# Two of the four operand sums made by adding transfers, with one quarter kept negated, in a one-core streaming-encoder block

## The chip, the cores and the metric

The kernel runs on one core of a Trainium2 chip. The metric is device time in microseconds (us) of one execution. Engine names follow the profile: PE is TensorE (matmul; PEld its weight loads), DVE is VectorE, ACT is ScalarE, POOL is GpSimd, SP is SyncE, which here only issues transfers. A transfer issued from SP is described by hardware, one issued from POOL by software, and only POOL's can add to their destination.

## The reference

One layer on x of 1024 tokens by 1024 channels, in float32, cut to what is computed:

```python
h = rmsnorm(x, norm_g)
q, k, v, za, u, vs, zs, gm = split(h @ w_in)
a   = window_sink_attention(rope(q), rope(k), v, sinks)
a   = (a * silu(za)) @ w_att_out
sgo = chunked_spatial_gating(gelu(u), gelu(vs), sg_w, sg_b, ln_g, ln_b)
sgo = (sgo * silu(zs)) @ w_sg_out
ga, gs = split(sigmoid(gm + b_merge))
out = rmsnorm(x + (ga * a + gs * sgo) @ w_o, final_g)
```

Below, "s" is the operand sgo * silu(zs) of w_sg_out, and "a" is the operand a * silu(za) of w_att_out. Both are matrices of 1024 by 1024.

## The kernel before, in words

**Products.** Every large product of a 1024 by 1024 operand goes by a seven-product scheme on halves (a Strassen scheme in Winograd's form). The operand is cut in four quarters q11, q12, q21, q22, and seven forms are made of them: b11, b21, b22 are quarters, t1 to t4 are sums of quarters. The other side, the weights, is cut and summed in the same way for each pair of 128-wide output blocks. Each float32 factor is split into a rounded high part and a remainder, and a product takes three matmuls (high by high, high by remainder, remainder by high) over four 128-blocks of the contraction: 12 matmuls of 128x512. `gemm_pair` (line 351) does one pair of output blocks with 7 x 12 = 84 matmuls, in the order b11, t1, t2, b21, t3, b22, t4. b11, t2, t3 and t4 go on in one PSUM bank (ps_mm): b11's product is copied out (the first x<-ps_mm copy, line 360), and then t2 is accumulated on top; so t2 can't start before that copy. t1 and b22 share a bank (ps_o) in the same way, with the copy of line 364 between them; b21 has its own (ps_tp).

**Splits.** `split` (line 147) has ScalarE round to the high part (a CAST, or an ACTIVATE with -1 where a form is negated) and VectorE subtract to get the remainder. A form of s or a is split by `fill_b` (line 179) in two halves of 128x1024 (tiles T_b11h, T_b11l and so on; each has one buffer). The weights of each pair are split into wh and wl, three buffers each, by `split_next` at set places of `gemm_pair`.

**Forms of s and a.** `forms_of` (line 1458) makes the seven forms of an operand whose quarters lie in the four bq tiles (128x4x512 each). It makes four sums on VectorE by `combine` (line 183), in place and in two halves each:

```python
combine(nc.vector.tensor_sub, q12, q11, q12)   # t1
combine(nc.vector.tensor_add, q12, q22, q12)   # t2, used with a minus sign
combine(nc.vector.tensor_sub, q11, q12, q11)   # t3
combine(nc.vector.tensor_sub, q21, q12, q21)   # t4
```

**Stages around the change.** Four pairs of h by za's weights come first (the stage called za here, starting at about 591 us; its last pair starts at 647.67). While they run, their outputs pass SiLU, are multiplied with the attention's output from at_dr (`finish_silu`, line 1550) and are stored to a_dr; and s is finished: zs is loaded, passes SiLU and is multiplied with rows of s1_dr (`parts_of_s`, line 1492, where a table of pair and hook sets what is done when; each pair has seven hooks). The first sum of s is made before the last za pair, the other forms during it, and four pairs of s by w_sg_out follow (from 666.71). During these, the quarters of a are loaded from a_dr, the outputs are multiplied with the sigmoid gate and stored to y_dr, and in the last pair the forms of a are made. Four pairs of a by w_att_out follow (from 748.56), and then the product with w_o by token.

**Gates.** The att gates (rows of at_dr) and the sigmoid gates (gs_dr, ga_dr) pass through 128x512 tiles named g0 to g3, one buffer each. In the za stage g0 and g1 hold att gates, and g2 and g3 hold rows of s1_dr for s.

**Order.** The program is written in one order, and a scheduler that estimates durations then sets each engine's instruction order, which the engine keeps to strictly. `after(second, first)` fixes an order between two instructions without a wait. Transfers from SP are issued in that queue's order, each behind the waits of those before it. In the za and s stages POOL's queue holds the stores to a_dr and y_dr.

Of the kernel before, what the change touches and what calls it, by code (L numbers as in the profile page):

```python
# [27 lines left out]
ALU = mybir.AluOpType  # L28
# [5 lines left out]
KC = D // P  # L34
# [18 lines left out]
def hybrid_tile(  # L53
# [16 lines left out]
    nc = tc.nc  # L70
# [55 lines left out]
    at_dr = scratch("at_dr")  # L126
# [3 lines left out]
    def rstd_of(ss, scale, base=EPS, n=1):  # L130
# [14 lines left out]
        nc.vector.tensor_mul(e[:], e[:], r0[:])  # L145
        return e

    def split(hi, lo, src, minus=False):
        if minus:
            nc.scalar.mul(hi, src, -1.0)  # L150
            nc.vector.scalar_tensor_tensor(
                lo, src, -1.0, hi.bitcast(F32), op0=ALU.mult, op1=ALU.subtract
            )
        else:
            nc.scalar.copy(hi, src)  # L155
            return nc.vector.tensor_sub(lo, src, hi.bitcast(F32))  # L156

    def after(second, first):

        tc.add_manual_dep(  # L160
            second.ins,
            first.ins.name,
            mybir.DependencyInfo(mybir.DependencyClass.NoSync, mybir.DependencyReason.DATA),
            reason="order",
        )
# [9 lines left out]
    def new_b(names=FORMS):  # L175
        return {n: (slot(n + "h"), slot(n + "l")) for n in names}

    def fill_b(b, name, src, minus=None):
        hi, lo = b[name]
        for c in range(0, 4, 2):  # L180
            split(hi[:, c : c + 2, :], lo[:, c : c + 2, :], src[:, c : c + 2, :], name == "t2" if minus is None else minus)

    def combine(op, dst, a, c):
        for i in range(0, 4, 2):
            op(dst[:, i : i + 2, :], a[:, i : i + 2, :], c[:, i : i + 2, :])  # L185

# [9 lines left out]
    def add_to(dst, src):  # L196
        nc.gpsimd.dma_start(dst, src, accum_op=ALU.add)

    def copy_to(dst, src):
        nc.sync.dma_start(dst, src)  # L200

    def begin_job():
        n = len(begun)
        if n < written[0]:
            begun.append(n)
            units.extend(jobs[n]())

    def split_next():

        if not units:  # L210
            begin_job()
        if not units:
            return
        halves, keys = units.pop(0)
        if keys[0][1] == 2:
            make_sums(term_of_x11[0] if done[0] <= 4 else None)
        hi = mtile([P, D], F32R, "wh", 3)
        lo = mtile([P, D], F32R, "wl", 3)
        if isinstance(halves, list):
            for c, half in enumerate(halves):  # L220
                split(hi[:, half_of(c)], lo[:, half_of(c)], half)
        else:
            wide = halves.shape[1]
            first = split(hi[:, 0:wide], lo[:, 0:wide], halves)
            if keys[0] == (done[0] - 1, 6) and done[0] > LAST_OF_Q + 2:
                make_sums(first)
        for c, key in enumerate(keys):
            ready[key] = hi[:, half_of(c)], lo[:, half_of(c)]
        if len(units) == 1:
            begin_job()  # L230

    def half_of(half):
        return slice(half * HALF, (half + 1) * HALF)
# [19 lines left out]
    def make_sums(first=None):  # L253

        while sums_to_make:
            sums_to_make.pop(0)(first)
# [73 lines left out]
    term = [None]  # L330
# [198 lines left out]
    casts, lows, turns = [], [], []  # L529
# [80 lines left out]
    def two_k(v, c):  # L610
        return v[:, 2 * c : 2 * c + 2, :]
# [131 lines left out]
    for c in range(2):  # L743
        hi, lo = (two_k(v, c) for v in s1_hl)
# [659 lines left out]
    QUARTERS = ((0, 0), (0, 1), (1, 0), (1, 1))  # L1404
# [51 lines left out]
            yield b  # L1456

    def forms_of(qs):
        q11, q12, q21, q22 = (qs[k] for k in QUARTERS)
        b = {}  # L1460

        def fill(name, q):
            b.update(new_b((name,)))
            fill_b(b, name, q)

        combine(nc.vector.tensor_sub, q12, q11, q12)
        yield
        fill("b11", q11)
        fill("t1", q12)
        combine(nc.vector.tensor_add, q12, q22, q12)  # L1470
        fill("t2", q12)
        fill("b21", q21)
        combine(nc.vector.tensor_sub, q11, q12, q11)
        fill("t3", q11)
        fill("b22", q22)
        combine(nc.vector.tensor_sub, q21, q12, q21)
        fill("t4", q21)
        yield b

    ORDER = ((0, 0), (1, 1), (0, 1), (1, 0))  # L1480
    gates = []

    turn = [0]

    def gtag(among=4):
        turn[0] += 1
        return f"g{turn[0] % among}"

    def want_gate(src, m, half, among=4):
        gates.append(get(src, m, half, 1, gtag(among)))  # L1490

    def parts_of_s():

        factors, of_rows = [], {}

        def rows(src, j, half):
            return src[:].rearrange("(c p) t -> p c t", p=P)[:, 4 * j : 4 * j + 4, half_of(half)]

        def load(j, half):
            s_q[j, half] = q = bq()
            copy_to(q[:], rows(z_dr, j, half))

# [12 lines left out]

        def load_row(c, half):
            of_rows[c, half] = get(s1_dr, 4 + c, half, 1, f"g{2 + c % 2}")

        def multiply_row(c, half):
            v = s_q[1, half][:, c, :]
            after(nc.vector.tensor_mul(v, v, of_rows[c, half][:]), term[0])

        return {
            (0, 1): [(load, 0, 0), (load_factors, 0, 0)],
            (0, 2): [(load, 1, 1)],
            (0, 3): [(load, 0, 1)],
            (0, 4): [(load_row, 0, 1), (load_row, 1, 1)],
            (0, 5): [(silu, 0, 0)],  # L1530
            (0, 6): [(multiply, 0, 0, 0)],
            (0, 7): [(multiply, 0, 0, 2), (load_factors, 0, 1), (silu, 1, 1)],
            (2, 1): [(multiply_row, 0, 1), (multiply_row, 1, 1), (load_row, 2, 1), (load_row, 3, 1)],
            (2, 3): [(silu, 0, 1)],
            (2, 6): [(multiply, 0, 1, 0), (multiply_row, 2, 1)],
            (2, 7): [(multiply, 0, 1, 2), (multiply_row, 3, 1), (load, 1, 0), (load_row, 0, 0), (load_row, 1, 0)],
            (4, 6): [(silu, 1, 0)],
            (4, 7): [(multiply_row, 0, 0), (multiply_row, 1, 0), (load_row, 2, 0), (load_row, 3, 0)],
            (6, 6): [(multiply_row, 2, 0), (multiply_row, 3, 0)],
        }  # L1540


    of_att = [(m + i, half) for m in range(0, KC, 2) for i, half in ORDER]
# [5 lines left out]

    def finish_silu(q, m, half):  # L1550

        after(nc.vector.tensor_mul(q[:], q[:], gates.pop(0)[:]), term[0])
        put(a_dr, m, half, q[:], nc.gpsimd)
        if of_att:
            want_gate(at_dr, *of_att.pop(0), 2)

    def part_of_s(m):
        of_za[0] += 1
# [5 lines left out]
    for m in range(0, KC, 2):  # L1564
        if m == 0:
            for _ in range(2):
                want_gate(at_dr, *of_att.pop(0), 2)
        if m == 6:
            s_forms = forms_of(s_q)
            next(s_forms)  # L1570

        def finish(i, half, q, src, sign):
            pace[0] = nc.scalar.activation(q[:], src, AF.Silu, scale=sign)
            silus.append((q, m + i, half))

        gemm_pair(hb, finish, lambda: part_of_s(m), "tp")
# [4 lines left out]

    def gate_of(src, m, i, half, col):

        g = gates.pop(0)
        c = col + m + i
        gate = nc.scalar.activation(g[:], g[:], AF.Sigmoid, bias=bm_sb[:, c : c + 1])

        after(gate, pace[0])
        return g
# [110 lines left out]
    fill = o_forms()  # L1700
# [211 lines left out]
```

## Time and profile before

| | us |
|---|---|
| median of three runs | 911.89 (910.78 to 914.15) |
| profiled execution, its own time | 912.14 |
| its span | 910.4 |
| TensorE busy | 894.2 |
| VectorE busy | 696.8 |
| ScalarE busy | 527.0 |
| POOL busy | 141.9 |

The mean granted TensorE clock of the profiled execution is 0.996. A timeline row gives start, duration, engine, line, operation, output and input, count (merged rows have x2), and in brackets the idle time of the engine before it and what ended that. Matmul records overlap, as they are pipelined: the distance between two starts says how fast they go, not the duration. Rows of windows give the busy time of each engine in a stretch with the count of instructions, then the granted clock, the share of the 16 transfer engines that was busy, and GB/s. A row of grouped instructions gives line, engine, operation, tiles, shape and count, then busy time and mean ns of one, then idle time before it. Rows of transfers end with the median us from issue to landing, where that is known.

### The profile page before, as it was taken

Reading aid. Unit: us, or ns where it says so; the run is one execution under the profiler, and the core shown is the slowest. Engines: PE = TensorE matmul, PEld = TensorE weight load, DVE = VectorE, ACT = ScalarE, POOL = GpSimd, SP = SyncE. Lnnn points to the kernel's source line nnn. Section 1 sums busy time; section 2 is a strip of 40 time slices with the busy share of each in tenths; the row PEclk is TensorE's granted clock in tenths of the full one; section 3 lists DMA queues with packets and bytes.
Section 4 is the critical chain, followed back from the end, with each engine's and each line's share of the span. In section 5 each row is a group of like instructions: output and inputs, shape, how many; then the busy total and the mean of one; then the engine's idle time right before and its main releaser. Section 6 shows DMA issues by size and latency. Waiting matters only on the chain.

```text
span 910.4 us, 13184 instructions
## 1 busy us (share of the span) xinstructions
PE 894.2 (98%) x4284; PEld 743.6 (82%) x4284; DVE 696.8 (77%) x1263; ACT 527.0 (58%) x1059; POOL 141.9 (16%) x204
## 2 busy tenths in 40 slices
PE   8999999999999999999999999999998999999996
PEld 6778888888878788888888888888877887888885
DVE  6869966666676788888878788657797489579986
ACT  7866533334545467767667677654674375367443
POOL 1322222203030001111111011201001111110012
PEclk9999999999999999999999999999999999999999
DMA  9997888858778767788786789899859665998632
GB/s 329 211 250 214 263 204 175 173 153 270 252 235 290 206 181 216 208 178 202 170 239 215 244 224 244 212 345 347 295 192 368 220 197 156 312 307 274 204 120 112
DMA packets 131598, 209.57 MB, mean 230 GB/s; under 512 B 12649, under 2 KB 61033, under 8 KB 131530
## 3 DMA queue, kind: packets, MB, share of 16 engines
q1 hardware_dynamic: 110072, 149.74, 49.7%
q0 software_dynamic: 21312, 58.73, 28.4%
q8 instruction: 34, 0.56, 0.3%
q14 instruction: 34, 0.28, 0.1%
q10 hardware_dynamic: 146, 0.27, 0.1%
HBM read 147.74 MB, written 86.11 MB: 257 GB/s over the span
## 4 chain that ended last, share of the span: by engine, by line
PE 87%; DVE 7%; DMA 2%; issue 1%; ACT 1%; SPq 0%; POOL 0%; DVEq 0%; ACTq 0%
PE ps_mm L342 36%; PE ps_o L342 26%; PE ps_sc L1242 3%; PE ps_tp L342 3%; PE ps_mm L669 3%; PE ps_tp L669 2%; PE ps_o L1327 2%; PE ps_sc L342 2%; PE ps_tp L1286 2%; PE ps_o L669 2%; PE ps_tp L917 2%; PE ps_sc L669 1%; DVE wl L156 1%; DVE bq L185 1%; DMA q_hl<-qhl 1%
## 5 line engine op out<-in xcount | busy, mean ns | idle before, releaser
L155 ACT CAST wh<-s 128x1024 fp32r<-128x1024 f32 (+1 forms) x79 | 79.2, 1005 | 96.0 <-PE ps_mm L342 52.0
L156 DVE TENSOR_TENSOR wl<-wr,wh 128x512 fp32r<-128x512 f32 (+1 forms) x77 | 72.0, 936 | 51.8 <-ACT wh L155 51.0
L156 DVE TENSOR_TENSOR wl<-s,wh 128x1024 fp32r<-128x1024 f32 (+1 forms) x79 | 92.5, 1171 | 12.3 <-ACT wh L155 12.1
L155 ACT CAST wh<-wr 128x512 fp32r<-128x512 f32 (+1 forms) x77 | 63.0, 820 | 58.4 <-PE ps_mm L342 30.4
L342 PE MATMUL ps_o<-T_t1h,wh 128*128 128x512 f32 x148 | 58.8, 397 | 0.8 <-ACT wh L155 0.7
L342 PE MATMUL ps_o<-T_b22h,wh 128*128 128x512 f32 x148 | 58.3, 394 | 0.0
L342 PE MATMUL ps_mm<-T_b11h,wl 128*128 128x512 f32 x140 | 55.4, 396 | 2.9 <-DVE wl L156 2.9
L342 PE MATMUL ps_o<-T_b22l,wh 128*128 128x512 f32 x148 | 57.9, 391 | 0.0
L342 PE MATMUL ps_o<-T_b22h,wl 128*128 128x512 f32 x148 | 57.7, 390 | 0.0
L342 PE MATMUL ps_o<-T_t1h,wl 128*128 128x512 f32 x148 | 57.7, 390 | 0.0
L342 PE MATMUL ps_o<-T_t1l,wh 128*128 128x512 f32 x148 | 57.6, 389 | 0.0
L1255 ACT ACTIVATE pr<-ps_sc,sm 128x192 f32<-128x192 f32 (+2 forms) x128 | 50.9, 410 | 9.0 <-DVE sm L1251 6.6
L342 PE MATMUL ps_mm<-T_b11h,wh 128*128 128x512 f32 x140 | 55.3, 395 | 0.0
L342 PE MATMUL ps_mm<-T_t4h,wh 128*128 128x512 f32 x140 | 55.3, 395 | 0.0
L342 PE MATMUL ps_mm<-T_t2h,wh 128*128 128x512 f32 x140 | 54.7, 391 | 0.6 <-ACT x L360 0.6
L342 PE MATMUL ps_mm<-T_t3l,wh 128*128 128x512 f32 x140 | 54.6, 390 | 0.6 <-DVE T_t3l L156 0.6
L342 PE MATMUL ps_mm<-T_b11l,wh 128*128 128x512 f32 x140 | 55.2, 394 | 0.0
L342 PE MATMUL ps_mm<-T_t3h,wh 128*128 128x512 f32 x140 | 54.9, 392 | 0.0
L342 PE MATMUL ps_mm<-T_t4h,wl 128*128 128x512 f32 x140 | 54.7, 391 | 0.0
L342 PE MATMUL ps_mm<-T_t3h,wl 128*128 128x512 f32 x140 | 54.7, 390 | 0.0
L342 PE MATMUL ps_mm<-T_t2h,wl 128*128 128x512 f32 x140 | 54.6, 390 | 0.0
L342 PE MATMUL ps_mm<-T_t2l,wh 128*128 128x512 f32 x140 | 54.6, 390 | 0.0
(389 smaller groups left out, 2395.2 us busy)
## 6 DMA issues: line engine op xcount, KB each, us to landing
wr<-in_w_dram SPq DMA_DIRECT2D x86, 256.0 KB
sums<-in_w_dram POOLq DMA_DIRECT2D x20, 512.0 KB, 6.7
s<-sums SPq DMA_DIRECT2D x20, 512.0 KB
q_hl<-qhl SPq DMA_DIRECT2D x16, 512.0 KB
q<-q_hl SPq DMA_DIRECT2D x64, 128.0 KB
y_dr<-x POOLq DMA_DIRECT2D x28, 256.0 KB, 6.5
g<-in_w_dram POOLq DMA_DIRECT2D x12, 512.0 KB, 6.0
wr<-in_w_dram SPq DMA_DIRECT2D x11, 512.0 KB
```

The costliest lines, as they stand in the source:

```text
L155: nc.scalar.copy(hi, src)
L156: return nc.vector.tensor_sub(lo, src, hi.bitcast(F32))
L185: op(dst[:, i : i + 2, :], a[:, i : i + 2, :], c[:, i : i + 2, :])
L342: nc.tensor.matmul(acc, lt, rt, start=fresh and k == 0 and n == 0, stop=k == 3 and n == 2, skip_group_check=True,)
L669: mm = nc.tensor.matmul(acc[:], lt, rt, start=fresh and k == 0 and n == 0, stop=k == 3 and n == 2, skip_group_check=True,)
L917: nc.tensor.matmul(pm[:, t * P : (t + 1) * P], xh[:, half * 4 + t, g * P : (g + 1) * P], bias[-1][1][:, g % 4, :], start=True, stop=True,)
L1242: nc.tensor.matmul(sc[:, i, k0:], q_of[:, c, i * P : (i + 1) * P], kt[:, f, k0:], start=f == 0, stop=f == 1,)
L1255: nc.scalar.activation(held_in[c, i], sc[:, i, lo:hi], AF.Exp, bias=nmax[:, c, i : i + 1], scale=-1.0, accum_out=sums[:, c, i : i + 1],)
L1286: nc.tensor.transpose(dst, pr[:, i, block * P : block * P + width], ident[:])
L1327: nc.tensor.matmul(po[:, cs], lt, rt, start=n == 0, stop=n == len(terms) - 1)
```

## The change

In `forms_of`, two of the four sums leave VectorE. t2's sum q12 + q22 and t4's sum are made by transfers on POOL's queue that add one SBUF tile to another, in halves of 128x1024 (`add_aside`, by `add_to`, the same helper that adds into y_dr). So that t4's sum q12 - q21 is an addition, q21 is kept negated from where it is multiplied: in `parts_of_s` for the quarter (1, 0) of s, in `finish_silu` for that of a. The new `times` multiplies with -1 in the same instruction. b21 is then split with a minus sign. The order of the forms changes: b21 is made before t2; the subtraction for t3 is put after t2's remainder, and t2's casts after a cast of the weights, by `after`.

The gate tiles g0 to g3 are handed out from a list of free ones in place of a running number. g2 and g3 join it for att gates at the second hook of the last za pair (`more_gates`), and the last two row products of s move there from that pair's sixth hook.

```diff
+    def times(v, by, minus):
+        if minus:
+            return nc.vector.scalar_tensor_tensor(v, v, -1.0, by, op0=ALU.mult, op1=ALU.mult)
+        return nc.vector.tensor_mul(v, v, by)

     def forms_of(qs):
-        q11, q12, q21, q22 = (qs[k] for k in QUARTERS)
+        q11, q12, minus21, q22 = (qs[k] for k in QUARTERS)
...
+        def add_aside(dst, src):
+            for i in range(0, 4, 2):
+                add_to(dst[:, i : i + 2, :], src[:, i : i + 2, :])
...
         fill("b11", q11)
         fill("t1", q12)
-        combine(nc.vector.tensor_add, q12, q22, q12)
-        fill("t2", q12)
-        fill("b21", q21)
-        combine(nc.vector.tensor_sub, q11, q12, q11)
+        add_aside(q12, q22)
+        fill("b21", minus21, True)
+        lows = fill("t2", q12)
+        for hi in hi_of[-2:]:
+            after(hi, of_units[-2])
+        add_aside(minus21, q12)
+        for sub in combine(nc.vector.tensor_sub, q11, q12, q11):
+            after(sub, lows[-1])
         fill("t3", q11)
         fill("b22", q22)
-        combine(nc.vector.tensor_sub, q21, q12, q21)
-        fill("t4", q21)
+        fill("t4", minus21)
...
-            after(nc.vector.tensor_mul(v, v, of_rows[c, half][:]), term[0])
+            after(times(v, of_rows[c, half][:], half == 0), term[0])
+
+        def more_gates():
+            free_tags.extend(("g2", "g3"))
+            for _ in range(2):
+                want_gate(at_dr, *of_att.pop(0))
...
-            (6, 6): [(multiply_row, 2, 0), (multiply_row, 3, 0)],
+            (6, 2): [(multiply_row, 2, 0), (multiply_row, 3, 0), (more_gates,)],
...
-        after(nc.vector.tensor_mul(q[:], q[:], gates.pop(0)[:]), term[0])
+        after(times(q[:], next_gate()[:], m >= KC // 2 and half == 0), term[0])
```

In the instruction order that results, VectorE has eight instructions fewer in all for the sums (four for s, four for a), and POOL eight adding transfers more. On TensorE, nine of the twelve b21 matmuls of the first s pair go before its t2 matmuls, and ahead of the first pair's t4 go five matmuls of the second pair's b11, where there were twelve of its b11, b21 and t1, for s and for a. On ScalarE, the casts of T_b21h go before those of T_t2h, and the casts of T_b22h and T_t4h go before those of T_t3h; in both stages T_t4h's casts now stand ahead of the first pair's copies out of ps_mm (b11) and ps_o (t1).

More of the change, by code (lines that the diff above doesn't have):

```diff
@@ L146, in rstd_of @@
         return e
+    hi_of = []
     def split(hi, lo, src, minus=False):
         if minus:
-            nc.scalar.mul(hi, src, -1.0)
-            nc.vector.scalar_tensor_tensor(
+            hi_of.append(nc.scalar.mul(hi, src, -1.0))
+            return nc.vector.scalar_tensor_tensor(
                 lo, src, -1.0, hi.bitcast(F32), op0=ALU.mult, op1=ALU.subtract
@@ L154, in split @@
         else:
-            nc.scalar.copy(hi, src)
+            hi_of.append(nc.scalar.copy(hi, src))
             return nc.vector.tensor_sub(lo, src, hi.bitcast(F32))
@@ L179, in fill_b @@
         hi, lo = b[name]
-        for c in range(0, 4, 2):
-            split(hi[:, c : c + 2, :], lo[:, c : c + 2, :], src[:, c : c + 2, :], name == "t2" if minus is None else minus)
+        minus = name == "t2" if minus is None else minus
+        return [
+            split(hi[:, c : c + 2, :], lo[:, c : c + 2, :], src[:, c : c + 2, :], minus) for c in range(0, 4, 2)
+        ]
     def combine(op, dst, a, c):
-        for i in range(0, 4, 2):
-            op(dst[:, i : i + 2, :], a[:, i : i + 2, :], c[:, i : i + 2, :])
+        return [op(dst[:, i : i + 2, :], a[:, i : i + 2, :], c[:, i : i + 2, :]) for i in range(0, 4, 2)]
     jobs = []
@@ L206, in begin_job @@
             units.extend(jobs[n]())
+    of_units = []
     def split_next():
@@ L226, in split_next @@
                 make_sums(first)
+        of_units.append(hi_of[-1])
         for c, key in enumerate(keys):
@@ L1458, in forms_of, with fill @@
     def forms_of(qs):
-        q11, q12, q21, q22 = (qs[k] for k in QUARTERS)
+        q11, q12, minus21, q22 = (qs[k] for k in QUARTERS)
         b = {}
-        def fill(name, q):
+        def fill(name, q, minus=None):
             b.update(new_b((name,)))
-            fill_b(b, name, q)
+            return fill_b(b, name, q, minus)
+        def add_aside(dst, src):
+            for i in range(0, 4, 2):
+                add_to(dst[:, i : i + 2, :], src[:, i : i + 2, :])
         combine(nc.vector.tensor_sub, q12, q11, q12)
@@ L1469, in forms_of, with gtag, want_gate, next_gate @@
         fill("t1", q12)
-        combine(nc.vector.tensor_add, q12, q22, q12)
-        fill("t2", q12)
-        fill("b21", q21)
-        combine(nc.vector.tensor_sub, q11, q12, q11)
+        add_aside(q12, q22)
[6 more added lines that the diff above has]
+            after(sub, lows[-1])
         fill("t3", q11)
         fill("b22", q22)
-        combine(nc.vector.tensor_sub, q21, q12, q21)
-        fill("t4", q21)
+        fill("t4", minus21)
         yield b
+    def times(v, by, minus):
+        if minus:
+            return nc.vector.scalar_tensor_tensor(v, v, -1.0, by, op0=ALU.mult, op1=ALU.mult)
+        return nc.vector.tensor_mul(v, v, by)
     ORDER = ((0, 0), (1, 1), (0, 1), (1, 0))
     gates = []
[L1483 to L1490, printed above, removed]
+    free_tags = ["g0", "g1"]
+    def gtag():
+        tag = free_tags.pop(0)
+        free_tags.append(tag)
+        return tag
+    def want_gate(src, m, half):
+        tag = free_tags.pop(0)
+        gates.append((tag, get(src, m, half, 1, tag)))
+    def next_gate():
+        tag, g = gates.pop(0)
+        free_tags.append(tag)
+        return g
     def parts_of_s():
@@ L1550, in finish_silu @@
     def finish_silu(q, m, half):
-        after(nc.vector.tensor_mul(q[:], q[:], gates.pop(0)[:]), term[0])
+        after(times(q[:], next_gate()[:], m >= KC // 2 and half == 0), term[0])
         put(a_dr, m, half, q[:], nc.gpsimd)
         if of_att:
-            want_gate(at_dr, *of_att.pop(0), 2)
+            want_gate(at_dr, *of_att.pop(0))
     def part_of_s(m):
@@ L1566, in hybrid_tile @@
             for _ in range(2):
-                want_gate(at_dr, *of_att.pop(0), 2)
+                want_gate(at_dr, *of_att.pop(0))
         if m == 6:
@@ L1582, in gate_of @@
     def gate_of(src, m, i, half, col):
-        g = gates.pop(0)
+        g = next_gate()
         c = col + m + i
```

## The prediction

> **What bounds the kernel now.** I read the page first: busy times and the chain of work that ended last.
>
> ```profile
> PE 894.2 (98%) x4284; PEld 743.6 (82%) x4284; DVE 696.8 (77%) x1263; ACT 527.0 (58%) x1059; POOL 141.9 (16%) x204
> PE 87%; DVE 7%; DMA 2%; issue 1%; ACT 1%; SPq 0%; POOL 0%; DVEq 0%; ACTq 0%
> ```
>
> TensorE bounds the whole, so time can only be won where it waits. The changed code makes the seven operand forms of s (used from 667 us on) and of a (from 749 us on), so next I read these two stretches: by windows, then TensorE's timeline.
>
> ```profile
> core 0: us, PE busy (x) PEld busy (x) DVE busy (x) ACT busy (x) POOL busy (x), PEclk, DMA share, GB/s
> 655.00:665.00 10.00, 10.00 (x46) 8.29 (x45) 10.00 (x11) 7.84 (x11) 0.54 (x1) 1.00 0.61 214
> 665.00:675.00 10.00, 10.00 (x46) 8.29 (x45) 8.90 (x12) 6.02 (x9) 1.62 (x3) 1.00 0.71 222
> 675.00:685.00 10.00, 9.37 (x41) 7.04 (x39) 10.00 (x10) 9.06 (x12) 0.00 (x0) 1.00 0.64 237
> 685.00:695.00 10.00, 7.54 (x26) 5.57 (x25) 9.28 (x12) 2.44 (x4) 1.62 (x3) 0.83 1.03 390
> 735.00:745.00 10.00, 10.00 (x46) 8.29 (x45) 9.64 (x12) 9.83 (x14) 0.54 (x1) 1.00 0.44 156
> 745.00:755.00 10.00, 10.00 (x46) 8.29 (x45) 10.00 (x11) 5.95 (x8) 1.63 (x3) 1.00 0.77 247
> 765.00:775.00 10.00, 8.84 (x38) 6.68 (x37) 8.85 (x11) 2.60 (x3) 3.51 (x4) 1.00 0.74 200
> ```
>
> In both stretches VectorE is full (10.00 of 10 us) before TensorE has its holes.
>
> ```profile
> 647.67 0.39 PE L342 MATMUL ps_mm<-T_b11h,wh 128*128 128x512 f32 x1
> 666.71 0.39 PE L342 MATMUL ps_mm<-T_b11h,wh 128*128 128x512 f32 x1
> 679.33 0.50 PE L342 MATMUL ps_mm<-T_t3l,wh 128*128 128x512 f32 x1 [0.63 <-DVE T_t3l L156]
> 686.00 0.50 PE L342 MATMUL ps_o<-T_t1h,wh 128*128 128x512 f32 x1 [0.71 <-ACT wh L155]
> 688.48 0.79 PE L342 MATMUL ps_mm<-T_b11h,wl 128*128 128x512 f32 x1 [1.75 <-DVE wl L156]
> 691.62 0.40 PE L342 MATMUL ps_mm<-T_t4l,wh 128*128 128x512 f32 x1
> 710.48 0.39 PE L342 MATMUL ps_mm<-T_b11h,wh 128*128 128x512 f32 x1
> 748.56 0.39 PE L342 MATMUL ps_mm<-T_b11h,wh 128*128 128x512 f32 x1
> 767.85 0.50 PE L342 MATMUL ps_mm<-T_b11h,wl 128*128 128x512 f32 x1 [1.10 <-DVE wl L156]
> 788.38 0.39 PE L342 MATMUL ps_mm<-T_b11h,wh 128*128 128x512 f32 x1
> ```
>
> A pair of output blocks is 84 matmuls. The last undisturbed one before the s forms runs from 647.67 to 666.71: 19.04 us, 0.2267 us a matmul. The first two pairs on the s forms start at 666.71 and end at 710.48: 43.77 us where two pairs take 38.08. So **5.69 us** are lost there. The first two on the a forms take 788.38 - 748.56 = 39.82 us: **1.74 us** lost. Together 7.43 us, which caps what the change can win. Part of it is the clock: from 688.48 to 691.62 seven matmul starts take 3.14 us instead of 1.59, and the windows show a granted clock of 0.83.
>
> **What ends these waits** is the VectorE backlog.
>
> ```profile
> L185 DVE TENSOR_TENSOR bq<-bq,bq 128x1024 f32<-128x1024 f32 x8 | 9.6, 1217 | 0.0
> L151 DVE SCALAR_TENSOR_TENSOR T_t2l<-bq,T_t2h 128x1024 fp32r<-128x1024 f32 x2 | 2.3, 1215 | 0.0
> 652.15 2.36 DVE L156 TENSOR_TENSOR T_b11l<-bq,T_b11h 128x1024 fp32r<-128x1024 f32 x2 [0.49 <-ACT T_b11h L155]
> 658.89 0.68 DVE L372 TENSOR_TENSOR x<-x,ps_tp 128x512 f32<-128x512 f32 x1
> 672.91 0.69 DVE L1552 TENSOR_TENSOR x<-x,g 128x512 f32<-128x512 f32 x1 [1.01 <-DMA g<-at_dr]
> 687.21 1.22 DVE L156 TENSOR_TENSOR wl<-wr,wh 128x1024 fp32r<-128x1024 f32 x1
> 736.73 2.36 DVE L156 TENSOR_TENSOR T_t1l<-bq,T_t1h 128x1024 fp32r<-128x1024 f32 x2 [0.36 <-ACT T_t1h L155]
> 740.74 0.68 DVE L372 TENSOR_TENSOR x<-x,ps_tp 128x512 f32<-128x512 f32 x1
> 766.58 1.21 DVE L156 TENSOR_TENSOR wl<-wr,wh 128x1024 fp32r<-128x1024 f32 x1
> ```
>
> The weight remainder wl that TensorE awaits at 688.48 is made at 687.21, at 767.85 the one made at 766.58; each stands in VectorE's order behind all of the forms' work.
>
> **The change, part by part.** Spacing on VectorE is 1.14 us for 128x1024 (two take 2.36) and about 0.60 for 128x512 (0.68 as in 658.89's row, less the same overlap of 0.08).
>
> (1) Removed: of the eight sums of each set of forms (four sums in two halves) four leave VectorE, 4 x 1.14 = 4.6 us for s and 4.6 us for a. The s wl of 687.21 then comes at 682.6 or earlier, and TensorE, undisturbed, needs it at 666.71 + (72 + 2) x 0.2267 = 683.5. The a wl of 766.58 comes at about 764.5, behind ScalarE's cast; it is wanted at 748.56 + 74 x 0.2267 = 765.3. Both holes close.
>
> (2) The gate loads. Two more buffers for the att gates from the second hook of the last za pair end the 1.01 us wait at 672.91, and four 128x512 row products move from about 667 to 653. The SP queue gets the same loads in another order; the two of s<-sums move behind gate loads:
>
> ```profile
> 670.20 0.53 SPq L200 DMA_DIRECT2D s<-sums  x1
> ```
>
> What they bring is first wanted at 666.71 + 96 x 0.2267 = 688.5, for t1 of the second pair, 18 us later. Nothing, by this cover; without it, each us of lateness over 10 or so would stall TensorE as long.
>
> (3) Negation: multiply with -1 and split with minus sign are a SCALAR_TENSOR_TENSOR in place of a TENSOR_TENSOR: 1215 beside 1217 ns. Nothing.
>
> (4) Added: eight adding transfers of 512 KB between SBUF tiles on POOL's queue. The same kind and size runs four times in the first stage:
>
> ```profile
> T_t3h<-T_t4h POOLq DMA_DIRECT2D x2, 512.0 KB, 6.9
> T_t3l<-T_t3h POOLq DMA_DIRECT2D x2, 512.0 KB, 4.9
> xh<-xh POOLq DMA_DIRECT2D x4, 256.0 KB, 10.1
> DMA to landing us min/median/max: 4.8/5.6/7.5
> 24.00:28.00 4.00, 4.00 (x23) 3.35 (x23) 2.57 (x8) 3.25 (x8) 0.86 (x1) 1.00 1.05 299
> 32.00:37.00 5.00, 5.00 (x25) 3.96 (x23) 4.27 (x13) 3.80 (x9) 1.81 (x3) 1.00 0.79 152
> ```
>
> From issue to landing L is 4.8 to 7.5 us (the fourth line is that of tile T_t3h, all four). The window with a DMA share of 1.05 holds the slowest, that of 0.79 the two fast ones. I take L = 6, near the mean of the four ((2 x 6.9 + 2 x 4.9) / 4 = 5.9); the ends are 4.8 and 7.5.
>
> (5) The order this brings. The changed instruction order puts ScalarE's two casts of t4, which need the second adding sum, ahead of x<-ps_mm, the copy of the b11 product that TensorE awaits before t2. That is the new wait.
>
> ```profile
> 664.01 1.05 ACT L155 CAST wh<-s 128x1024 fp32r<-128x1024 f32 x1 [0.54 <-ACT x L1573]
> 664.96 1.99 ACT L155 CAST T_b22h<-bq 128x1024 fp32r<-128x1024 f32 x2
> 669.84 0.58 ACT L360 COPY x<-ps_mm 128x512 f32<-128x512 f32 x1
> 748.71 1.05 ACT L155 CAST wh<-s 128x1024 fp32r<-128x1024 f32 x1
> ```
>
> ScalarE spaces such casts by 0.95 us (two take 1.99). For s: from 664.01 come wh, two t2, wh, two b22 (six casts) and two activations of 0.5, then t4 twice: the second may start at 671.7. After it follow t3 and the copy: 671.7 + 0.95 + 0.95 + 0.6, and 0.2 until TensorE sees it: 674.4. TensorE now runs nine b21 matmuls before t2 and is there at 666.71 + 33 x 0.2267 = 674.2. The loss is 0.2, with what I can't resolve 0.4 us. For a: from 748.71 wh, two b22, two t4 and the copy: 748.71 + 5 x 0.95 + 0.6 + 0.2 = 754.3 against 748.56 + 24 x 0.2267 = 754.0; I put 0.5.
>
> Does the transfer land in time? For s, t1's second half is done at 652.15 + 4 x 1.14 + 3 x 0.60 = 658.5 (two row products and one wl come between). The first sum's second half lands at 658.6 + L. The second sum starts when that and the split of b21 are done (658.89 + 3 x 1.14 + 3 x 0.60 = 664.1), so lands at 658.7 + 2L, or 664.2 + L for L under 5.5. It must be there by 671.7: true up to L = 6.5. For a, t1 is done at 739.1, b21 at 740.74 + 5.2 = 746.0; the second sum is needed at 752.5: landing at 739.2 + 2L or 746.1 + L, true up to L = 6.5. At L = 6 neither waits. POOL's a_dr and y_dr stores queue behind these waits by some 1 to 2 us; their next readers come later by more than 10 us.
>
> **The sum** against the profiled execution (912.14 us; span 910.4): s wins 5.69 - 0.4 = 5.3, a wins 1.74 - 0.5 = 1.2, together 6.5 us. 912.1 - 6.5 = **905.6 us**; against the median of 911.89 it would be 905.4, no difference here.
>
> **Rivals.** A: the adding transfers land slowly, about 7.5 us. Then t4 lands at 673.7 (2.0 us behind its turn, so s loses 0.4 + 2.0 = 2.4) and at 754.2 (1.6 behind, so a loses 2.1): the win is 7.4 - 4.5 = 2.9, 909.2 us. For it: each of the transfers brings its own load to a DMA share of 0.61, 0.71, 0.44 and 0.77. Against: 0.79 already included two of them in 5 us. The Trainium skill, "DMA: Bandwidth & Descriptors", section "Issuing engines are not separate DMA queues", says that transfers of all queues share 16 engines and interleave; by that rule POOL's transfers slow down beside SP's loads, which is this case and 909.2. The two windows, 1.05 with the 7.5 us and 0.79 with 4.9, agree with it. Should such holes lower the clock as at 688.48, another 3.14 - 1.59 = 1.55 us goes at each: 912.3. The Trainium skill, "TensorE: Matmul & The Clock Gate", section "What's actually happening", has the clock fall only after an idle window of about 3.4 us; by it A stays at 909.2. The trace differs: 1.75 us of idle time, with 0.63 and 0.71 before, was followed by the slow matmuls.
>
> B, slower: the same ScalarE order with L near 10, which xh<-xh shows (10.1 us). Both holes grow by 2 us for each us of L: together 4L - 25.4, so the change pays nothing from L = 8.2 and costs 0.5% from about 9.3. At 10: 14.6 - 7.4 = 7.2 us more, 919.3 us. Against it: no transfer of this form took over 7.5.
>
> C: VectorE's 4.6 us are not what held TensorE, and loads or ScalarE end the waits at the same places; then 911 to 913. Against: both holes name wl on VectorE, and ScalarE is 24% busy from 685 to 695.
>
> **How the numbers follow.** 0.5% of 912 is 4.6 us, about what a measurement of this kernel can tell from no change. My forecast 0.57 (own range 904.5 to 907.5: from all 7.4 won to L slightly over 6.5), A 0.22, C 0.07, B 0.14. Faster by over 0.5% 0.57, within 0.29 (A and C), slower 0.14. The range is 904.3 to 912.5: all won, with 0.4 of scatter, up to A with the clock's price; it leaves B out.
>
> **What the profile after would show.** Right: no L185 rows for the t2 and t4 sums, POOL bq<-bq landing in under 6.5 us, clock 1.00 from 670 to 700, first two pairs of each set within 0.5 us of 38.08. Wrong: ScalarE idle before T_t4h on a DMA, TensorE waiting for x (L366 there) at t2, or a hole on wl as before.

## The result, and the profile after

| | before | after |
|---|---|---|
| median, us (5 runs each, beside each other) | 910.94 | **924.84** (924.47 to 925.83) |
| ratio to before, 95% interval | | 1.0145 (1.0132 to 1.0159) |
| span of the profiled execution, us | 910.4 | 922.7 |
| mean granted TensorE clock | 0.996 | 0.989 |

The change made the kernel 1.45% slower; 905.6 us were predicted, 0.6% below the median before. The page after, its busy line and the group of matmuls that waits longest:

```profile
PE 896.2 (97%) x4284; PEld 746.2 (81%) x4284; DVE 688.6 (75%) x1255; ACT 527.0 (57%) x1059; POOL 149.4 (16%) x212
L348 PE MATMUL ps_mm<-T_t2h,wh 128*128 128x512 f32 x140 | 56.6, 404 | 13.9 <-ACT x L366 13.9
```

VectorE did lose work (688.6 us of busy time against 696.8: eight sums gone). But TensorE now waits 13.9 us at t2, for ScalarE's copy of the b11 product (L366, in the kernel before L360). TensorE's timeline gives the place: the first matmul of each stretch, as in the prediction, and every wait of over 0.2 us between them.

```profile
646.99 0.39 PE L348 MATMUL ps_mm<-T_b11h,wh 128*128 128x512 f32 x1
664.78 0.50 PE L348 MATMUL ps_mm<-T_t4h,wh 128*128 128x512 f32 x1 [1.31 <-DVE x L383]
667.63 0.39 PE L348 MATMUL ps_mm<-T_b11h,wh 128*128 128x512 f32 x1
682.34 0.79 PE L348 MATMUL ps_mm<-T_t2h,wh 128*128 128x512 f32 x1 [7.06 <-ACT x L366]
715.75 0.39 PE L348 MATMUL ps_mm<-T_b11h,wh 128*128 128x512 f32 x1
753.83 0.39 PE L348 MATMUL ps_mm<-T_b11h,wh 128*128 128x512 f32 x1
766.30 0.80 PE L348 MATMUL ps_mm<-T_t2h,wh 128*128 128x512 f32 x1 [6.88 <-ACT x L366]
800.79 0.39 PE L348 MATMUL ps_mm<-T_b11h,wh 128*128 128x512 f32 x1
```

The old holes on the weight remainder wl are gone. In their place stand two of 7 us and a small new one in the last za pair. From one start to the next:

| stretch | before | after | of it, holes | more than undisturbed |
|---|---|---|---|---|
| last za pair | 19.04 | 20.64 | 1.31 | 1.60 |
| first two s pairs | 43.77 | 48.12 | 7.06 | 10.04 (before 5.69) |
| first two a pairs | 39.82 | 46.96 | 6.88 | 8.88 (before 1.74) |

This is the whole of it: 1.60 + (10.04 - 5.69) + (8.88 - 1.74) = 13.09, less 0.68 because the stretch begins earlier (646.99 against 647.67), is 12.41; the a stretch ends at 800.79 against 788.38, 12.41 later, and the spans differ by 12.3.

What ScalarE does before the first hole, and before the second (its timeline):

```profile
674.50 1.05 ACT L157 CAST T_t4h<-bq 128x1024 fp32r<-128x1024 f32 x1
679.81 1.04 ACT L157 CAST T_t4h<-bq 128x1024 fp32r<-128x1024 f32 x1 [4.26 <-DMA bq<-bq]
680.76 1.04 ACT L157 CAST T_t3h<-bq 128x1024 fp32r<-128x1024 f32 x1
681.71 0.58 ACT L366 COPY x<-ps_mm 128x512 f32<-128x512 f32 x1
759.07 1.05 ACT L157 CAST T_t4h<-bq 128x1024 fp32r<-128x1024 f32 x1 [0.56 <-DMA bq<-bq]
764.72 1.04 ACT L157 CAST T_t4h<-bq 128x1024 fp32r<-128x1024 f32 x1 [4.61 <-DMA bq<-bq]
765.67 0.58 ACT L366 COPY x<-ps_mm 128x512 f32<-128x512 f32 x1
```

ScalarE stands idle in front of the second cast of t4 until the adding transfer has landed; the copy that TensorE needs stands behind it in the order. The adding transfers themselves, in the rows of transfers for 640 to 720 us and 735 to 790 us (last number: median us from issue to landing):

```profile
bq<-bq POOLq DMA_DIRECT2D x4, 512.0 KB, 7.8
bq<-bq POOLq DMA_DIRECT2D x4, 512.0 KB, 8.8
```

One by one they land 7.2, 8.4, 6.5 and 9.1 us after their issue for s, and 6.3, 9.1, 8.5 and 9.6 for a: a mean of 8.1, where 6 was assumed.

The clock adds to each hole. Windows from the end of the holes (columns: window, its length, busy time and count of PE, PEld, DVE, ACT and POOL, granted clock, share of the transfer engines, GB/s):

```profile
682.30:685.00 2.70, 2.66 (x6) 2.15 (x7) 2.50 (x3) 1.43 (x2) 0.00 (x0) 0.50 0.72 212
685.00:688.00 3.00, 3.00 (x8) 2.31 (x7) 2.89 (x3) 0.52 (x1) 0.00 (x0) 0.50 1.01 371
688.00:691.00 3.00, 3.00 (x14) 2.44 (x13) 1.29 (x2) 2.97 (x5) 0.00 (x0) 0.99 1.06 400
766.30:769.95 3.65, 3.65 (x9) 2.91 (x10) 2.23 (x2) 2.33 (x3) 0.00 (x0) 0.50 0.11 43
```

For 5.7 us after the first hole TensorE gets a clock of 0.50, so half of that, some 2.8 us, is lost; 10.04 - 7.06 = 2.98 is what the pairs lost beside the hole. At the second it is 3.65 us at 0.50, some 1.8 us, of 8.88 - 6.88 = 2.00.

### The profile page after: what moved, and what is told of

It reads as the page before. It is cut to its first block, busy times and chain, and to the rows that moved or that the text cites. A ratio compares the mean times of both kernels' runs of the same rounds, so it can differ in the third digit from the quotient of the medians.

```text
span 922.7 us, 13208 instructions
## 1 busy us (share of the span) xinstructions
PE 896.2 (97%) x4284; PEld 746.2 (81%) x4284; DVE 688.6 (75%) x1255; ACT 527.0 (57%) x1059; POOL 149.4 (16%) x212
## 5 line engine op out<-in xcount | busy, mean ns | idle before, releaser
L348 PE MATMUL ps_mm<-T_t2h,wh 128*128 128x512 f32 x140 | 56.6, 404 | 13.9 <-ACT x L366 13.9
L348 PE MATMUL ps_o<-T_t1h,wh 128*128 128x512 f32 x148 | 58.6, 396 | 0.0
L348 PE MATMUL ps_o<-T_b22h,wh 128*128 128x512 f32 x148 | 58.3, 394 | 0.0
L348 PE MATMUL ps_o<-T_b22l,wh 128*128 128x512 f32 x148 | 57.8, 391 | 0.0
L348 PE MATMUL ps_o<-T_b22h,wl 128*128 128x512 f32 x148 | 57.7, 390 | 0.0
L348 PE MATMUL ps_o<-T_t1h,wl 128*128 128x512 f32 x148 | 57.7, 390 | 0.0
L348 PE MATMUL ps_o<-T_t1l,wh 128*128 128x512 f32 x148 | 57.6, 389 | 0.0
L348 PE MATMUL ps_mm<-T_t4h,wh 128*128 128x512 f32 x140 | 55.1, 394 | 1.3 <-DVE x L383 1.3
L348 PE MATMUL ps_mm<-T_t2l,wh 128*128 128x512 f32 x140 | 56.3, 402 | 0.0
L348 PE MATMUL ps_mm<-T_t2h,wl 128*128 128x512 f32 x140 | 56.1, 401 | 0.0
L348 PE MATMUL ps_mm<-T_t3h,wh 128*128 128x512 f32 x140 | 54.9, 392 | 0.0
L348 PE MATMUL ps_mm<-T_b11h,wh 128*128 128x512 f32 x140 | 54.9, 392 | 0.0
L348 PE MATMUL ps_mm<-T_t4h,wl 128*128 128x512 f32 x140 | 54.7, 391 | 0.0
L348 PE MATMUL ps_mm<-T_b11l,wh 128*128 128x512 f32 x140 | 54.7, 391 | 0.0
L348 PE MATMUL ps_mm<-T_b11h,wl 128*128 128x512 f32 x140 | 54.7, 390 | 0.0
L348 PE MATMUL ps_mm<-T_t3h,wl 128*128 128x512 f32 x140 | 54.7, 390 | 0.0
L348 PE MATMUL ps_mm<-T_t4l,wh 128*128 128x512 f32 x140 | 54.5, 390 | 0.0
```

What stands on the lines that cost most here:

```text
L348: nc.tensor.matmul(acc, lt, rt, start=fresh and k == 0 and n == 0, stop=k == 3 and n == 2, skip_group_check=True,)
```

## The experiments

Each edit is to the changed kernel unless said otherwise; ratios are to the kernel before, run on the same chip. Lengths are those of the last za pair, of the first two s pairs and of the first two a pairs (undisturbed 19.04, 38.08, 38.08).

| run | median us | ratio, 95% interval | za | s | a |
|---|---|---|---|---|---|
| t4's casts behind t3's | 911.06 | 0.9999 (0.9988 to 1.0010) | 20.83 | 41.06 | 40.12 |
| sums on VectorE | 912.21 | 1.0013 (1.0002 to 1.0024) | 20.78 | 41.22 | 39.83 |
| rows later | 920.64 | 1.0110 (1.0088 to 1.0133) | 19.04 | 46.07 | 46.29 |
| plain copies | 908.02 | 0.9962 (0.9947 to 0.9976) | 21.00 | 39.41 | 38.25 |
| t4 and rows late | 907.16 | 0.9949 (0.9935 to 0.9963) | 19.04 | 39.84 | 39.75 |
| t4 late | 911.89 | 0.9999 (0.9988 to 1.0009) | 20.37 | 42.03 | 39.97 |
| half by transfer | 913.18 | 1.0018 (1.0003 to 1.0034) | 22.70 | 38.60 | 43.08 |
| t2's sum on VectorE | 922.90 | 1.0124 (1.0109 to 1.0139) | 22.31 | 45.07 | 45.95 |
| t4 and rows late, y stores on SP | 906.69 | 0.9938 (0.9917 to 0.9959) | 19.04 | 38.40 | 38.69 |
| the same, a stores too | 906.85 | 0.9944 (0.9923 to 0.9966) | 19.04 | 39.25 | 38.78 |

### Is it ScalarE's order? t4's casts behind t3's

```diff
         fill("t3", q11)
+        last_of_t3 = hi_of[-1]
         fill("b22", q22)
         fill("t4", minus21)
+        for hi in hi_of[-2:]:
+            after(hi, last_of_t3)
```

> T_t4h's casts are ordered behind T_t3h's, so that in ScalarE's order the copies of the b11 and t1 products (and t3) stand ahead of the casts that wait for the second adding sum. Theory ORDER (TensorE's 13.9 us of waiting for that copy are the whole loss): both waits go; what is left is the late t4 itself, some 2 us in each stage, and 1.6 us in the last za pair: 909 to 913 us. Rival LATE FORMS (the adding transfers land so late that TensorE waits anyway, now at t4): under 4 us won, 920 us or more.

911.06 us: 13.8 us of the 13.9 by which the medians differ come back, by an edit that moves two casts of ScalarE. The transfers still land in 5.8 to 9.5 us. TensorE's waits (columns: total, times, longest):

```profile
PE ps_mm L348 <- ACT x L373: 2.2, 2, 1.6
PE ps_mm L348 <- ACT x L366: 1.7, 1, 1.7
PE ps_mm L348 <- DVE x L383: 1.5, 1, 1.5
```

So the loss needs a copy that stands behind a slow transfer. Both waits were expected to go, and for s 1.7 us stay at L366: there the second cast of t2 waits 1.56 us for the first adding sum, and the copy stands behind that. The other 2.2 us wait for the next copy, x12 (L373, which takes ps_mm out after t2, and which t3 awaits); it now stands behind the casts of t4.

### All four sums back on VectorE

```diff
-            for i in range(0, 4, 2):
-                add_to(dst[:, i : i + 2, :], src[:, i : i + 2, :])
+            combine(nc.vector.tensor_add, dst, dst, src)
```

> The changed kernel with its two sums made on VectorE again (negation, gates, row products and the order of the forms stay as changed). Theory ADDS (only the adding transfers cost): within 1 us of the kernel before, 910 to 912. Rival REST (the moved row products and the form order cost too): 1.6 us of the za pair stay and more, 913 us or more.

912.21 us, the time before within 0.24%, and 0.2 us above the range of ADDS. This kernel keeps the kept negation, the extra gate buffers and the early row products; together they win nothing, and the 20.78 us of the last za pair show a loss, as REST had it. Without transfers in its way the scheduler put the copies ahead of t4's casts, so this run doesn't measure the transfers alone. Its waits on wl are back (2.0 us in two), as before.

### The row products and gates two hooks later

```diff
-            (6, 2): [(multiply_row, 2, 0), (multiply_row, 3, 0), (more_gates,)],
+            (6, 4): [(multiply_row, 2, 0), (multiply_row, 3, 0), (more_gates,)],
```

> The changed kernel with the last two row products and the two gate buffers two hooks later (fourth instead of second hook of the last za pair). Theory EARLY ROWS (VectorE's 3.3 us wait for the s1 rows comes from multiplying before the load has landed, and delays the first sum): that wait goes, t1's remainder is done some 4 us earlier, the first two adding transfers start near 656 us, the za pair takes 19.04 us again, and the t4 landing in s moves up by 1 to 3 us: 919 to 922 us. Rival: the wait moves on with the rows, 924 us.

920.64 us, 4.2 less than the change. The last za pair is undisturbed again. In the changed kernel VectorE's timeline shows why it wasn't:

```profile
655.96 1.29 DVE L1495 SCALAR_TENSOR_TENSOR bq<-bq,g 128x512 f32<-128x512 f32 x2 [3.26 <-DMA g<-s_dr]
660.05 1.22 DVE L158 TENSOR_TENSOR T_t1l<-bq,T_t1h 128x1024 fp32r<-128x1024 f32 x1
```

At (6, 2) the rows of s1_dr have not arrived: VectorE stands still for 3.26 us, and all behind it comes later, t1's second remainder (done at 661.3 instead of the 658.5 of the prediction) and with it the first adding transfers. With the rows later the holes at t2 are still 5.10 and 6.49 us.

### Adding or only crowding: plain copies in place of the adding transfers

```diff
-                add_to(dst[:, i : i + 2, :], src[:, i : i + 2, :])
+                nc.gpsimd.dma_start(dst[:, i : i + 2, :], src[:, i : i + 2, :])
```

The copies overwrite their destination, so t2 and t4 are made of one quarter and not of the sum; the sums of these two are left out.

> The changed kernel with the eight adding transfers replaced by plain copies of the same size between the same tiles, on the same queue and behind the same waits (the sums of t2 and t4 are left out). Theory CROWDING (the landing time comes from the 16 transfer engines being full): landing stays at 7 to 9 us, time within 3 us of the changed kernel, 922 to 925. Rival ADDING (reading the destination makes it slow): landing 4 to 5.5 us, 911 to 916 us.

908.02 us, below the 911 to 916 of the rival ADDING. Same tiles, same size, same queue, same places; the landing of the four for s and the four for a:

```profile
bq<-bq POOLq DMA_DIRECT2D x4, 512.0 KB, 4.5
bq<-bq POOLq DMA_DIRECT2D x4, 512.0 KB, 4.3
```

The share of the transfer engines was 0.67 to 1.00 from issue to landing, against 0.82 to 1.05 with the adding ones. That small difference isn't the reason: at a share of 0.94 to 1.00 plain copies landed in 4.2 to 6.1 us, and at 0.82 adding ones in 6.3 and 7.2. What makes them slow here is the adding. And with transfers that land in 6.1 us at the latest, s (39.41) and a (38.25) win nearly what the prediction had forecast; with the za pair undisturbed the time would be, by my estimate, 908.02 - (21.00 - 19.04) = 906.1.

### Both causes taken away

t4 is split only at the third hook of the first pair, behind the copy x12, and the rows come two hooks later.

```diff
         fill("b22", q22)
+        yield b
         fill("t4", minus21)
-        yield b
+        for hi in hi_of[-2:]:
+            after(hi, pace[0])
+        yield
...
+            if m == 0 and at[0] == 3:
+                next(forms)
...
-            (6, 2): [(multiply_row, 2, 0), (multiply_row, 3, 0), (more_gates,)],
+            (6, 4): [(multiply_row, 2, 0), (multiply_row, 3, 0), (more_gates,)],
...
```

> Edit to the changed kernel: the row products and the two extra att gates start two hooks later, and the two casts of t4 are issued only after ScalarE's copy x12 of the first pair, so no copy that TensorE awaits stands behind an adding transfer. Theory TWO CAUSES (copies behind the t4 casts, and VectorE waiting for rows that are asked for too early): the last za pair returns to 19.0 us, the first two s pairs take 38.5 to 39.5 and the first two a pairs 38.2 to 39.2, landings stay at 6 to 9.7 us and matter no longer; 904 to 907 us. Rival THIRD CAUSE (the slow transfers also hold the t2 casts or VectorE's own chain): a wait for t2 or for a weight remainder is left, 909 to 912.

907.16 us, faster than before by 0.51% (0.37 to 0.65), and 0.2 us above the range expected. Two causes it is, with a rest: s and a took 39.84 and 39.75, above the 38.5 to 39.5 and 38.2 to 39.2 expected. In a most of the rest is a wait at t3 for the copy x12, and that copy stood for something else than a cast (TensorE's and ScalarE's timeline):

```profile
757.69 0.50 PE L348 MATMUL ps_mm<-T_t3h,wh 128*128 128x512 f32 x1 [1.33 <-ACT x L373]
757.05 0.59 ACT L373 COPY x<-ps_mm 128x512 f32<-128x512 f32 x1 [2.58 <-DMA y_dr<-x]
```

The copy's target, one of the five x tiles, was still being stored to y_dr, from POOL's queue, where the adding transfers are. That store was issued at 747.27, 0.5 us behind the last adding transfer, and landed at 756.98, 1.2 us after that transfer.

### t4's casts late alone

The same edit without the (6, 4) line.

> Edit: only the two casts of t4 go after the copy x12 of the first pair; the row products stay early. TWO CAUSES: s and a pairs as above (38.5 to 39.5 and 38.2 to 39.2), but the last za pair keeps 20.6 to 20.9 us; 905.5 to 909. Against the run with the casts behind t3 (911.06) this measures the copy x12 behind the casts. THIRD CAUSE: 910 to 912.

911.89 us, a miss: 905.5 to 909 was expected, and the 910 to 912 of THIRD CAUSE came. The early rows cost more than the za pair shows. With VectorE 3 us behind, the first adding transfers start at 659.93 and 661.92 instead of 657.07 and 658.20, so the casts of t2 are late too, as that rival had it, and the copy of b11 behind them:

```profile
PE ps_mm L348 <- ACT x L373: 2.5, 2, 1.6
PE ps_mm L348 <- ACT x L366: 1.6, 1, 1.6
PE ps_mm L348 <- DVE x L383: 1.2, 2, 1.0
```

The waits for x12 (L373) are about as long as with the casts behind t3, though no cast of t4 stands ahead of it now. ScalarE's timeline gives another reason, in both stages: the copy's target is still being stored.

```profile
681.08 0.59 ACT L373 COPY x<-ps_mm 128x512 f32<-128x512 f32 x1 [2.21 <-DMA a_dr<-x]
759.88 0.59 ACT L373 COPY x<-ps_mm 128x512 f32<-128x512 f32 x1 [3.02 <-DMA y_dr<-x]
```

Against the run with both edits, s lost 2.2 us and the za pair 1.3.

### Why do they land late? Half of each sum

```diff
-            for i in range(0, 4, 2):
-                add_to(dst[:, i : i + 2, :], src[:, i : i + 2, :])
+            nc.vector.tensor_add(dst[:, 0:2, :], dst[:, 0:2, :], src[:, 0:2, :])
+            add_to(dst[:, 2:4, :], src[:, 2:4, :])
```

> Edit to the changed kernel: the first half of each of the two sums goes back to VectorE, only the second half is an adding transfer, so four of 512 KB are left and no two run at once. Theory PAIRS (the second of two adding transfers is slow because it runs beside the first): each of the four lands in 5 to 6.8 us. Rival ALONE TOO (the load of the other queues alone makes them slow): 8 to 9.5 us. Time with PAIRS 906 to 911, with ALONE TOO 911 to 916; the last za pair stays at 20.6 to 21.

913.18 us, in the range of the rival, with 22.70 us for the za pair where 20.6 to 21 was expected; and the time settles nothing about the landing: for s the single transfers took 4.8 and 5.8 us, as the theory of pairs has it, for a 8.3 and 7.0. Nor does the share of the transfer engines tell them apart. The windows from issue to landing of the second of s and the first of a:

```profile
668.20:674.00 5.80, 5.80 (x21) 4.65 (x21) 5.43 (x7) 5.21 (x7) 1.92 (x3) 0.78 0.97 219
738.00:746.30 8.30, 8.30 (x39) 6.86 (x38) 8.20 (x11) 6.55 (x9) 1.44 (x2) 1.00 0.85 214
```

The slower one had the lower share, 0.85 against 0.97. What differs is when the first packet moves. The first of a was issued at 738.01; the queues' rows for 738 to 741.5 us and 741.5 to 744.3 (q0 is POOL's queue, q1 SP's: packets, MB, share of the transfer engines' time) are

```profile
q1 hardware_dynamic: 91, 0.37, 61.7%
q0 software_dynamic: 128, 0.50, 89.6%
```

POOL's queue moves nothing in the first 3.5 us, while SP's does, and then 0.50 of its 0.52 MB in 2.8 us. The first of s, issued at 662.16 and landed in 4.8 us, has all its 0.52 MB moved between 663.5 and 666.1. Why POOL's queue sometimes gets its turn so late stays open.

### One landing alone

```diff
-        add_aside(q12, q22)
+        combine(nc.vector.tensor_add, q12, q12, q22)
```

> Edit to the changed kernel: the t2 sum goes back to VectorE (2.3 us in each set), t4's stays an adding transfer. Theory CHAIN (the second sum is late because it stands behind the first): with the first gone the second is issued when VectorE has split b21, at about 665 and 750, and lands by 674 and 758; waits of TensorE on copies fall from 7 to under 3 us for each set; 909 to 914. Rival LANDING ALONE (one landing of 8 to 9.6 us is enough to hold the copy): waits stay above 4 us in each set; 917 to 921.

922.90 us, above the 917 to 921 of the rival, but its waits hold. t4's two transfers were issued at 669.62 and 673.69 and landed after 5.6 and 9.5 us, at 683.1 and not by 674; for a, after 5.9 and 10.0. With t2's transfers gone the second half is still the late one, though issued only 1.6 us before the first landed (1.0 us for a). The scheduler had put only the copy of b11 ahead of the second cast, so now x12 waited behind it:

```profile
PE ps_mm L348 <- ACT x L373: 8.2, 2, 5.1
PE ps_mm L348 <- DVE x L383: 2.9, 1, 2.9
PE ps_mm L348 <- ACT x L366: 1.0, 1, 1.0
```

One late landing is enough, whichever copy stands behind it.

### The stores out of POOL's queue

To the kernel with t4 and rows late:

```diff
-            put(y_dr, m + i, half, q[:], nc.gpsimd)
+            put(y_dr, m + i, half, q[:], nc.sync if m == 6 else nc.gpsimd)
```

> Edit to the run with t4 and rows late (907.16): the four y_dr stores of the last s pair are issued from SP instead of POOL; ScalarE's order is the same. There ScalarE's copy x12 of the first a pair stood idle for 2.58 us on such a store, and TensorE waited 1.33 us. Theory STORE BEHIND THE ADDS (the store holds an x buffer because POOL's queue gives it its turn only after the adding transfers): the wait at t3 of the first a pair goes, the first two a pairs take 38.1 to 38.6 instead of 39.75, landings of the a sums stay 6 to 9.2 with ends 3.5 to 5 us apart; 905.3 to 906.5. Rival STORE SLOW ANYWHERE (SP's loads ahead of it hold it as long): the wait stays within 0.5 us of 1.33, 906.8 to 908.

906.69 us, faster than before by 0.62% (0.41 to 0.83), the lowest median here, though not told apart from 907.16; its profiled execution took 904.12. The wait of 1.33 us is gone; of matmul waits of the seven-product scheme (L348) this one is left, where the changed kernel has 15.2 us:

```profile
PE ps_mm L348 <- DVE x L383: 0.2, 1, 0.2
```

a took 38.69, 0.1 above what was expected; the time is 0.2 above.

```diff
-        put(a_dr, m, half, q[:], nc.gpsimd)
+        put(a_dr, m, half, q[:], nc.sync if m >= 6 else nc.gpsimd)
```

> Edit to the same run: the four a_dr stores of the last za pair go to SP as well, so POOL's queue holds nothing but the adding transfers in both stretches. Theory ONE AT A TIME (adding transfers of one queue are served one after another, 3.4 to 5 us each, so the second of two issued together lands late whatever else the queue holds): landings of first sums' halves still 6 to 7 and 9 to 9.7, those of the second sums 6 to 9. Rival STORES IN BETWEEN (the 256 KB stores in the same queue made the later ones slow): all but the second land in 5 to 6.5. Time 905 to 907 by either; 908 to 911 if the loads of weight sums, which now stand behind the a_dr stores on SP, come late.

906.85 us. Nothing but adding transfers is now issued from POOL from 656 to 668 us and from 733 to 746, and they land no sooner:

```profile
bq<-bq POOLq DMA_DIRECT2D x4, 512.0 KB, 8.7
bq<-bq POOLq DMA_DIRECT2D x4, 512.0 KB, 9.4
```

One by one 6.6, 9.1, 8.3 and 9.7, then 6.2, 10.1, 8.8 and 10.8. The stores in between are not the cause. From these landings and the issue times the transfers end at 663.3, 666.9, 673.2, 677.1 and 740.2, 745.2, 749.5, 756.5, never less than 3.6 us apart; the first two plain copies ended 1.4 us apart (664.9 and 666.3). That fits adding transfers served one at a time, and the packets show it. The first two of the changed kernel were issued at 659.83 and 661.82; the rows of POOL's queue there, for 657 to 666.1 us and 666.1 to 669.6, and then with plain copies, for 736 to 738 us:

```profile
q0 software_dynamic: 133, 0.52, 28.9%
q0 software_dynamic: 152, 0.52, 75.5%
q0 software_dynamic: 142, 0.52, 65.4%
```

By 666.1 the queue has moved the 0.52 MB of one transfer, and the same again in the 3.5 us behind that: the second half waits for the first. Each adding transfer takes 2.6 us of all 16 engines (28.9% of 9.1 us, 75.5% of 3.5 us), the plain copy 1.3 us (65.4% of 2.0 us) for as many bytes. It isn't all: the last one here took 7.0 us after the one before it had ended, and the single ones of the half-sum run took anything from 4.8 to 8.3; there a late start added to the landing.

## Why the prediction was wrong, step by step

**What bounds the kernel; step (1), the sums off VectorE: right.** Both holes on wl are gone in the changed kernel, and where the transfers land by 6.1 us s and a come within 1.33 and 0.17 us of undisturbed. The cap of 7.43 us was sound: with y's stores on SP, s loses 0.32 and a 0.61 of it, and the medians differ by 5.2 us.

**Step (2), rows and gates at nothing: wrong.** The prediction looked at the queue of loads and at what TensorE needs 18 us later, and not at whether the moved products' own rows have arrived. They hadn't: VectorE waits 3.26 us, the za pair loses 1.60, and t1 is split 2.8 us later than the working had it. With the rows later the adding transfers of s are issued 3.6 to 4.9 us sooner. Undone alone, this gives 4.2 us back.

**Step (3), the negation at nothing:** no run takes it apart, and nothing speaks against it. With all sums on VectorE, VectorE's busy time is 697.0 against 696.8.

**Step (4), the landing at L = 6: the step that failed.** It measured 6.3 to 9.6, mean 8.1; no first landing was under 6.3 and the second of a pair was never under 8.4. The four rows of the first stage (4.8 to 7.5) gave ends for the range that don't contain the mean here. The 10.1 us of xh<-xh stood quoted beside them and was set aside as another form. And L was taken as one number for every transfer, where the second half of a sum took 1.0 to 2.8 us longer than the first, as it waits for the first's 2.6 us of all 16 engines.

**Step (5), the new wait: right in mechanism.** The casts of t4 stand ahead of the copy L366 and TensorE waits there, at t2 in both first pairs; only the size was wrong, as no wait was expected at L = 6. The limit of L = 6.5 fits: the plain copies stayed under it, and their waits at L366 add up to 0.9 us. That POOL's stores queue behind and harm nobody was wrong by 1.33 us in the run with t4 and rows late, and by 2.5 us with t4 late alone: not the next reader of y_dr or a_dr was hurt, but the x tile that the store holds.

**The rivals.** It went as B, which had 0.14. Its formula for both holes with the landing of the second halves, (8.4 + 9.1 + 9.1 + 9.6) / 4 = 9.05, gives 4 x 9.05 - 25.4 = 10.8 us; measured were 7.06 + 6.88 = 13.9, and 5.10 + 6.49 = 11.6 with the rows later, so some 2.3 of the 3.1 us above the formula go with the early rows of step (2). B left out the clock, 2.98 + 2.00 = 5.0 us, which A had at 1.55 for each hole; after holes of 7 us it is up to twice that. Rival A's limit was set by the same rows as step (4), and C fell with step (1).

The Trainium skill's "DMA: Bandwidth & Descriptors", section "Issuing engines are not separate DMA queues", was read as speaking for A, but by crowding alone the plain copies, at a share of 0.94 to 1.00 in five of eight, would have landed as late as the adding transfers; the trace shows a mean of 4.6 us for the eight against 8.1. The rule of the Trainium skill's "TensorE: Matmul & The Clock Gate", section "What's actually happening", that only an idle window of about 3.4 us lowers the clock, agrees with the holes of 6.88 and 7.06 us, followed by 0.50, and with 1.72 us (t4's casts behind t3's), followed by 1.00. It disagrees with 1.90 and 2.75 us (half by transfer, up to 666.18 and 755.53), both followed by 0.50, the first four rows here; and 2.93 us (t2's sum on VectorE, up to 667.39) was followed by 1.00, the next two:

```profile
663.95:667.36 3.41, 1.51 (x7) 1.01 (x6) 3.41 (x5) 2.12 (x3) 0.34 (x1) 1.00 0.96 209
667.36:670.77 3.41, 3.41 (x10) 2.63 (x9) 3.41 (x6) 2.83 (x5) 1.36 (x3) 0.50 0.81 223
752.70:756.11 3.41, 0.66 (x3) 0.48 (x3) 3.41 (x4) 2.16 (x4) 0.00 (x0) 1.00 0.98 376
756.11:759.52 3.41, 3.41 (x9) 2.63 (x8) 1.52 (x2) 1.75 (x2) 0.00 (x0) 0.50 0.62 243
664.46:667.39 2.93, 0.00 (x1) 0.01 (x1) 2.93 (x5) 1.60 (x3) 0.00 (x0) 1.00 0.21 68
667.39:670.80 3.41, 3.41 (x15) 2.80 (x16) 3.41 (x5) 3.41 (x5) 1.42 (x2) 1.00 0.49 168
682.68:686.09 3.41, 0.40 (x1) 0.19 (x1) 0.90 (x1) 2.92 (x4) 0.00 (x0) 1.00 0.92 288
686.09:689.50 3.41, 3.13 (x8) 2.45 (x8) 3.21 (x4) 3.38 (x5) 0.00 (x0) 0.50 0.66 214
```

So the length of a hole alone doesn't decide. In the half-sum run the clock changes at 667.36, 670.77, 756.11 and 759.52, each a whole number of 3.41 us apart (1, 25 and 1), as if each such stretch set the clock of the next; the two ahead of the falls hold 1.90 and 2.75 us of idle time. In the run with t2's sum on VectorE the clock falls at 686.09 (the last two rows), and six times 3.41 us before that is 665.6, inside the hole of 2.93 us, which so falls into 1.15 and 1.78 us. That is a reading of these holes; no run was made to test it.

## What to carry to other kernels

Work taken from a busy engine and given to a transfer gets a landing time that the busiest rows of the trace must price, not the mean ones, and for several in one queue from the end of the one before. Then look in each engine's order for what stands behind the first instruction that reads the result: here two casts could be late without harm, and the copy behind them could not. A step moved earlier must be asked first whether its own inputs are there.

## What the runs showed of the hardware that was not expected

- An adding transfer of 512 KB between two SBUF tiles landed in 8.1 us on average (changed kernel, eight of them), a plain copy of the same tiles at the same places in 4.6 (eight of them). The adding one took 2.6 us of all 16 transfer engines for its 0.52 MB, the plain one 1.3.
- The second half of a sum, issued 1.1 to 5.4 us behind the first half on the same queue, took 8.2 to 10.9 us in every run with adding transfers of both halves, with or without stores in between; first halves took 5.4 to 9.4, single ones (half by transfer) 4.8 to 8.3.
- A store that waits its turn behind adding transfers holds its source tile: ScalarE stood idle for 2.58 us before its copy into it, and moving four stores to SP ended that.
- A hole of TensorE of 1.90 us was followed by 3.41 us at a granted clock of 0.50, and one of 2.93 us by none.
